# Hybrid decoder step: RWKV chain with full-array products and a block diagonal state, the last merge's gates issued behind the delta pair, the norm's mean taken from PSUM

## The chip, the cores and the metric

The kernel runs on one core of one Trainium2 chip. A core has five engines with instruction streams of their own: TensorE (PE, with PEld for its weight loads), VectorE (DVE), ScalarE (ACT), GpSimd (POOL) and SyncE (SP), which here issues the DMAs. The metric is the device time of one execution, in microseconds, the median of the runs; lower is better.

## What is computed

One inference step of a decoder with two layers, 512 prompt positions and 8 samples of 8 positions, together 576 columns, 1024 channels, float32.

```python
for l in range(DEPTH):                                    # 2
    x = layer_norm(ALPHA * x + 0.5 * swiglu(x, ffn1_w_in, ffn1_w_out))
    mix = token_mixing(x, ...)
    x = layer_norm(ALPHA * x + mix)
    x = layer_norm(ALPHA * x + 0.5 * swiglu(x, ffn2_w_in, ffn2_w_out))

# token_mixing: four branches read one projection of x
oa, ob, oc, om = rwkv7(pa), pool(pb), delta(pc), memory_attention(pm)
for i, o in enumerate((oa, ob, oc, om)):
    merged += sigmoid(pg[i]) * (o @ w_branch[i])
mix = merged @ w_out

# rwkv7, for each of 8 heads of 64 channels, over the positions
def step(s, inp):
    r_t, w_t, k_t, v_t, kk_t, a_t = inp
    sa = einsum('bhvk,bhk->bhv', s, kk_t)
    s = s * w_t - sa * (kk_t * a_t) + v_t * k_t
    return s, einsum('bhvk,bhk->bhv', s, r_t)
```

The delta branch has a recurrence of the same family, with heads of 128.

## The kernel before

Activations lie with channels on the partitions and the 576 columns along the free axis, in two halves of 288. Each dense product is made in split precision: a weight block of 128x512 is loaded by SyncE, cast by ScalarE to `fp32r` (L239) and its remainder formed by VectorE (L241); `mms` (L255) then issues three 128x288 products per block of 128 channels, 24 for eight blocks, 12 for four. There are 17,952 such products in a run.

A tile scheduler sets the order of each engine's stream from the program's dependencies. The program offers it two kinds of work: the chains of the branches, and **fill**, dense products that a generator (`fill_steps`, taken on by `advance`) hands out between the steps of the chains: the pool branch, attention, and the four merges of the branches. A merge (`merge`) makes for each of eight channel blocks j and each half a gate (24 products `pgt`, then a tanh into `th`), multiplies the branch with its `w_branch` (12 products `pbr`), and adds the two's product to `merged`. Merges come in the order i=1, then rows 12, 0 and 8 of the branch outputs; row 8, the delta branch, is the last and can start only when the second delta pair has stored its output in DRAM (`od`) and read it back (`oraw`, split into `O`). One gate is made ahead of its first `pbr`.

The RWKV branch runs over four pairs of heads, p = 0 to 3. `rwkv_prep` makes the tiles of a pair: `KR` holds for each chunk of 64 positions the scaled kk and r (L827, L828), `KB` the other factors (L825, L832); `pt` (L845) are their products, masked on VectorE into `MA` (L846); `inverse64` inverts the triangular part into a tile `W`. `rwkv_chain` then goes through eight chunks in turn. In each, `pr` sums `MA` times `VS` (the values) and `KR` times the state `S` (L916, L917), `rhs` is its copy on VectorE (L922), `psa` is the inverse times `rhs` (L891 in `rwkv_solve`), ScalarE writes it negated into `VS` (L893), `pu` is `KN` times `VS` (L929), from which VectorE makes the next `S` (L937); `pyc` collects the output (L921, L932), copied by ScalarE (L939). All of it is cut by head: two 64x64 or 128x64 products for each term. Between the steps, `rwkv_sample` hands out the steps of the samples' group (`pst`, `psel`, `pr8`, `py8`, `pu8`), one after the right-hand side, one after the solution or one at the chunk's end.

The delta branch (`delta_pair`, q = 0, 1) has a chain of its own (`pdz` L1258, `pdo` L1264, `pdu` L1284, L1328, `pdk`), ends with a norm on VectorE and ScalarE (`dVN`) and transposes the output by `pto` (L1356), after which `stash` stores it.

Each of the six norms (`out_norm`) collects statistics per half: at block j = 3 (`statistics`) the first four blocks are summed, `pm` is the product with ones, ScalarE scales it into `m` (L309), VectorE subtracts `m` from four blocks (L313), GpSimd subtracts it from later ones (L288). At the end VectorE makes the diagonals `dg` (L353) from which TensorE makes `prow` (L363).

## Time and profile before

| | |
|---|---|
| median of three runs | 3206.25 us (3206.08 to 3207.3) |
| the profiled execution | 3201.57 us |
| its span | 3199.9 us |
| mean granted clock of TensorE | 0.982 |
| TensorE busy | 3065.8 us, 96% |
| VectorE busy | 1934.4 us, 60% |
| ScalarE busy | 1283.6 us, 40% |
| GpSimd busy | 502.7 us, 16% |

The span is from the first to the last instruction of the profiled execution. Busy times are shares of that span; since products are pipelined, a busy TensorE also counts the overlap of its products. The timeline gives each instruction's start; the distance between starts is what a product takes from the stream.

### The profile page before, as it was taken

Reading aid. Unit: us, or ns where it says so; the run is one execution under the profiler, and the core shown is the slowest. Engines: PE = TensorE matmul, PEld = TensorE weight load, DVE = VectorE, ACT = ScalarE, POOL = GpSimd, SP = SyncE. Lnnn points to the kernel's source line nnn. Section 1 sums busy time; section 2 is a strip of 40 time slices with the busy share of each in tenths; the row PEclk is TensorE's granted clock in tenths of the full one; section 3 lists DMA queues with packets and bytes.
Section 4 is the critical chain, followed back from the end, with each engine's and each line's share of the span. In section 5 each row is a group of like instructions: output and inputs, shape, how many; then the busy total and the mean of one; then the engine's idle time right before and its main releaser. Section 6 shows DMA issues by size and latency. Waiting matters only on the chain. (4 is left out here: it accounts for less than half of the span.)

```text
span 3199.9 us, 61758 instructions
## 1 busy us (share of the span) xinstructions
PE 3065.8 (96%) x24224; PEld 2840.4 (89%) x24224; DVE 1934.4 (60%) x4405; ACT 1283.6 (40%) x3057; POOL 502.7 (16%) x819
## 2 busy tenths in 40 slices
PE   7999999999999989999999999999999998999998
PEld 7999988778888889899999998876888897989998
DVE  4335776466687756733673367775586887475337
ACT  3332544434535333432343235445345343344323
POOL 2002221102110114200220022211111101142002
PEclk9999999999999999999999999999999999999999
DMA  4232432142233233322332233322322332333222
GB/s 131 84 89 84 112 101 58 38 119 61 61 88 85 66 93 97 90 84 82 103 101 83 80 99 92 109 55 71 93 63 64 84 91 67 95 96 92 87 79 77
DMA packets 509902, 271.88 MB, mean 85 GB/s; under 512 B 45896, under 2 KB 500140, under 8 KB 509612
## 3 DMA queue, kind: packets, MB, share of 16 engines
q1 hardware_dynamic: 509612, 267.95, 30.4%
q8 instruction: 190, 3.11, 0.4%
q14 instruction: 100, 0.82, 0.1%
HBM read 248.12 MB, written 19.76 MB: 84 GB/s over the span
## 5 line engine op out<-in xcount | busy, mean ns | idle before, releaser
L241 DVE TENSOR_TENSOR w<-raw,w 128x512 fp32r<-128x512 f32 (+1 forms) x824 | 601.8, 733 | 371.8 <-ACT w L239 367.1
L239 ACT CAST w<-raw 128x512 fp32r<-128x512 f32 (+1 forms) x824 | 503.0, 614 | 642.3 <-PE po L255 233.8
L255 PE MATMUL pp<-X,w 128*128 128x288 f32 x3552 | 534.9, 303 | 7.2 <-ACT pv L555 2.8
L255 PEld LDWEIGHTS pp<-X,w 128*128 128x128 f32 x3552 | 485.8, 189 | 28.9 <-issue 11.8
L255 PE MATMUL pgt<-X,w 128*128 128x288 f32 x3072 | 505.6, 308 | 5.7 <-ACT th__29684 L1597 2.2
L255 PEld LDWEIGHTS pgt<-X,w 128*128 128x128 f32 x3072 | 433.2, 191 | 24.9 <-issue 7.9
L255 PE MATMUL pg<-X,w 128*128 128x288 f32 x3072 | 445.9, 297 | 5.4 <-DVE X L274 3.3
L255 PE MATMUL pu<-X,w 128*128 128x288 f32 x3072 | 438.5, 295 | 0.0
L255 PEld LDWEIGHTS pg<-X,w 128*128 128x128 f32 x3072 | 420.6, 189 | 10.7 <-DVE X L274 6.5
L255 PEld LDWEIGHTS pu<-X,w 128*128 128x128 f32 x3072 | 418.8, 188 | 0.1
L255 PE MATMUL po<-H,w 128*128 128x288 f32 x3072 | 414.0, 296 | 0.0
L255 PEld LDWEIGHTS po<-H,w 128*128 128x128 f32 x3072 | 409.6, 188 | 1.3
L255 PE MATMUL pbr<-O,w 128*128 128x288 f32 x1344 | 234.2, 310 | 23.9 <-ACT w L239 18.3
L255 PEld LDWEIGHTS pbr<-O,w 128*128 128x128 f32 x1344 | 193.7, 192 | 33.2 <-ACT w L239 21.2
L451 DVE TENSOR_TENSOR h<-h,pu 128x288 f32<-128x288 f32 x128 | 58.0, 453 | 259.5 <-PE pu L255 258.4
L288 POOL TENSOR_TENSOR T<-T,m 128x288 f32<-128x288 f32 x48 | 48.0, 1030 | 932.2 <-ACT m L309 931.9
L273 ACT CAST H<-h 128x288 fp32r<-128x288 f32 x128 | 55.2, 432 | 193.9 <-DVE h L451 193.8
L450 ACT ACTIVATE h<-pg 128x288 f32<-128x288 f32 x128 | 52.7, 411 | 179.2 <-PE pg L255 175.1
L255 PE MATMUL po<-mh,w 128*128 128x288 f32 x768 | 109.3, 304 | 4.3 <-DVE w L241 2.9
L255 PEld LDWEIGHTS po<-mh,w 128*128 128x128 f32 x768 | 106.6, 195 | 6.0 <-DVE w L241 3.3
L286 POOL TENSOR_TENSOR T<-X 128x288 f32<-128x288 f32 x96 | 92.3, 995 | 83.7 <-DVE X L274 55.3
L645 DVE TENSOR_TENSOR it<-W,iu 128x60 f32<-128x60 f32 (+24 forms) x372 | 96.3, 259 | 8.6
(1030 smaller groups left out, 3652.9 us busy)
## 6 DMA issues: line engine op xcount, KB each, us to landing
raw<-in_w_in_dram SPq DMA_DIRECT2D x280, 256.0 KB
raw<-in_ffn_w_in_dram SPq DMA_DIRECT2D x272, 256.0 KB
raw<-in_ffn_w_out_dram SPq DMA_DIRECT2D x160, 256.0 KB
raw<-in_w_branch_dram SPq DMA_DIRECT2D x48, 256.0 KB
raw<-in_w_out_dram SPq DMA_DIRECT2D x48, 256.0 KB
oraw<-od SPq DMA_DIRECT2D x28, 288.0 KB
kraw<-in_mem_w_kv_dram SPq DMA_DIRECT2D x16, 256.0 KB
kvr<-in_cache_mem_k_dram SPq DMA_DIRECT2D x16, 256.0 KB
```

Source lines behind the costliest of these rows:

```text
L239: nc.scalar.copy(w[:, 0, :m], raw)
L241: low.tensor_sub(w[:, 1, :m], raw, w[:, 0, :m].bitcast(F32))
L255: self.last = self.nc.tensor.matmul(ps, w[:, wp, d, :], X[k][:, part, sl], start=first and k == 0 and q == 0, stop=last and k == n - 1 and ...
L273: nc.scalar.copy(out[:, 0, sl], src)
L286: nc.gpsimd.tensor_add(t, self.X[j][:, 0, sl].bitcast(F32), self.X[j][:, 1, sl].bitcast(F32))
L288: nc.gpsimd.tensor_sub(t, t, self.stat[s]['m'])
L450: nc.scalar.activation(h, pg, AF.Silu)
L451: nc.vector.tensor_mul(h, h, pu)
L645: nc.vector.tensor_mul(w, d[:, :r, k:k + 1].to_broadcast([P, r, m]), u[:, k + 1:, k].unsqueeze(1).to_broadcast([P, r, m]))
```

## The change

Three things are changed.

**The RWKV chain.** The state of a head pair is one 128x128 tile `sb`, block diagonal, whose zeros are written once; the right-hand side goes into such a tile too, `rb`. `KR`'s two parts change places for the second head, so that the part of one head and the other's zero blocks fit the full product. The masked products are sorted into two tiles: `ML` for those with kk, `MR` for those with r; the inverse is written over the matrices in `ML`, and no tile `W` is used. `VS` gets zeros in its off-diagonal blocks from GpSimd. Each chunk then has six 128x128 products in place of its 64-wide ones. On the other engines an operation that covered both heads is two, one for each diagonal block: the copy into `rb`, the update of `sb`, the copy of `pyc`, and in the prep the writing of `KR` and the masking. The three kinds of sample steps all come at the chunk's end, and the sample group's own solution and output use the full products too. The final state is transposed whole.

**The last merge.** For row 8, five gates are made ahead instead of one; their products are issued only behind the last transpose `pto` (`self.pin`), and their `th` come from another tag of the pool.

**The norm's mean.** At j = 3 the four subtractions read the sum in PSUM, scaled in the same instruction, and not `m`; `m` is still made for GpSimd.

```diff
+        self.sb, self.rb = c.tile([P, P], F32, name="sb"), c.tile([P, P], F32, name="rb")
+        for t in (self.sb, self.rb):
+            nc.gpsimd.memset(t, 0.0)
...
+            for t in t4:
+                nc.vector.scalar_tensor_tensor(t, pz, -2.0 / D, t, ALU.mult, ALU.add)
         for i in range(0 if j == 3 else j, j + 1):
             ti = self.T[i // 2][:, i % 2, sl]
-            if i < 4:
-                nc.vector.tensor_sub(ti, ti, st['m'])
...
-        nc.vector.scalar_tensor_tensor(KR[:, :, 0], ch(k), col('rwkv_k_k'), ch(e1), ALU.mult, ALU.mult)
-        nc.vector.tensor_mul(KR[:, :, 1], ch(r), ch(ec2))
+
+        for h in range(2):
+            nc.vector.scalar_tensor_tensor(KR[R[h], :, 1 - h], ch(k)[R[h]], col('rwkv_k_k')[R[h]], ch(e1)[R[h]],
+                                           ALU.mult, ALU.mult)
+            nc.vector.tensor_mul(KR[R[h], :, h], ch(r)[R[h]], ch(ec2)[R[h]])
...
-                nc.vector.tensor_mul(MA[h][:, c:c + m].rearrange("p c k t -> p c (k t)"),
-                                     pt[:, :m * P].rearrange("p (c t) -> p c t", t=P),
-                                     mk.unsqueeze(1).to_broadcast([P, m, P]))
+                for kind, (dst, at) in enumerate(((ML, 1 - h), (MR, h))):
+                    nc.vector.tensor_mul(dst[:, c:c + m, at],
+                                         pt[:, :m * P].rearrange("p (c k t) -> p c k t", k=2, t=64)[:, :, at],
+                                         mk[:, 64 * kind:64 * kind + 64].unsqueeze(1).to_broadcast([P, m, 64]))
...
+        for h in range(2):
+            nc.gpsimd.memset(VS[R[h], :, R[1 - h]], 0.0)
...
-        DT = self.inverse64(lambda h: MA[h][R[1 - h], :, 0], lambda h: 64 * (1 - h))
+
+        DT = lambda h: ML[R[1 - h], :, 1 - h]
+        self.inverse64(DT, lambda h: 64 * (1 - h), DT)
...
+            nc.vector.tensor_copy(self.rb[R[1 - h], R[h]], rhs(h))
         psa = self.bank("psa")
-        for h in range(2):
-            nc.tensor.matmul(psa[R[1 - h], :64], DT[R[1 - h], c], rhs[R[1 - h]], start=True, stop=True)
-        for h in range(2):
-            nc.scalar.mul(VS[R[1 - h], c, R[h]], psa[R[1 - h], :64], -1.0)
+        nc.tensor.matmul(psa[:, :P], ML[:, c].rearrange("p k t -> p (k t)"), self.rb, start=True, stop=True)
+        for h in range(2):
+            nc.scalar.mul(VS[R[1 - h], c, R[h]], psa[R[1 - h], R[h]], -1.0)
...
+            nc.tensor.matmul(pr[:, :P], flat(ML[:, c]), VS[:, c], start=True, stop=c == 0)
+            if c:
+                nc.tensor.matmul(pr[:, :P], flat(KR[:, c]), S, start=False, stop=True)
+                nc.tensor.matmul(py[:, :P], S, flat(KR[:, c]), start=True, stop=False)
+            self.rwkv_solve(parts, c, lambda h: pr[R[1 - h], R[h]])
+            pu = self.bank("pu")
+            nc.tensor.matmul(pu[:, :P], KN[:, c], VS[:, c], start=True, stop=True)
+            nc.tensor.matmul(py[:, :P], VS[:, c], flat(MR[:, c]), start=c == 0, stop=True)
             for h in range(2):
-                if S is not None:
-                    nc.tensor.matmul(pr[R[1 - h], :64], KR[R[h], c, 0], S[R[h]], start=True, stop=False)
-                nc.tensor.matmul(pr[R[1 - h], :64], MA[h][R[h], c, 0], VS[R[h], c, R[h]], start=S is None,
-                                 stop=True)
-            if S is not None:
-                for h in range(2):
-                    nc.tensor.matmul(py[R[h], :64], S[R[h]], KR[R[h], c, 1], start=True, stop=False)
-            nc.vector.tensor_copy(rhs, pr[:, :64])
-            sample_step("wide")
-            self.rwkv_solve(parts, c, rhs)
-            sample_step("solve")
-            pu = self.bank("pu")
+                d = S[R[h], R[h]]
+                if c:
+                    nc.vector.scalar_tensor_tensor(d, d, pc[R[h], c:c + 1], pu[R[h], R[h]], ALU.mult, ALU.add)
+                else:
+                    nc.vector.tensor_copy(d, pu[R[h], R[h]])
             for h in range(2):
-                vs = VS[:, c, 64 * h:64 * h + 64]
-                nc.tensor.matmul(pu[R[h], :64], KN[:, c, 64 * h:64 * h + 64], vs, start=True, stop=True)
-            for h in range(2):
-                vs = VS[:, c, 64 * h:64 * h + 64]
-                nc.tensor.matmul(py[R[h], :64], vs, MA[h][:, c, 1], start=S is None, stop=True)
-            Sn = self.scr.tile([P, 64], F32, tag="S64", name="S64", bufs=2)
-            if S is None:
-                nc.vector.tensor_copy(Sn, pu[:, :64])
-            else:
-                nc.vector.scalar_tensor_tensor(Sn, S, pc[:, c:c + 1], pu[:, :64], ALU.mult, ALU.add)
-            S = Sn
-            nc.scalar.copy(y[:, 64 * c:64 * c + 64], py[:, :64])
-            sample_step("deep")
+                nc.scalar.copy(y[R[h], 64 * c:64 * c + 64], py[R[h], R[h]])
+            for kind in ("wide", "solve", "deep"):
+                sample_step(kind)
...
+                self.pin = nc.tensor.transpose(pt[:, d * P:(d + 1) * P], ON[:, c0 + d], self.ident)
...
-            self.mms(pg, gates[j], self.X, HALVES[s])
-            th = self.half("th_", "xf") if dst is None else dst
+            with self.tc.issue_after(self.pin.ins) if row == 8 else nullcontext():
+                self.mms(pg, gates[j], self.X, HALVES[s])
+            th = self.half("th_", "x" if row == 8 else "xf") if dst is None else dst
...
-            while todo and len(ahead) < (1 if j == 0 else 0):
+            while todo and len(ahead) < (0 if j else 5 if row == 8 else 1):
```

Line numbers grow by 3 to 14: L255 is L259 in the changed kernel, L241 is L245, L1356 is L1359.

TensorE in one chunk of the first head pair's chain, before (names as above; `pp` and `pgt` on L255 are fill):

```order
L916 MATMUL pr<-S_5618,KR 64x64
L917 MATMUL pr<-VS,MA_4376 64x64
L916 MATMUL pr<-S_5618,KR 64x64
L917 MATMUL pr<-VS,MA_4377 64x64
L921 MATMUL pyc<-KR,S_5618 64x64 x2
L255 MATMUL pp<-X,w 128x288 x2
L891 MATMUL psa<-rhs,W 64x64 x2
L255 MATMUL pp<-X,w 128x288 x5
L929 MATMUL pu<-VS,KN 64x64 x2
L932 MATMUL pyc<-MA_4376,VS 64x64
L932 MATMUL pyc<-MA_4377,VS 64x64
```

The same chain after (L929 to L932 make `pr` and `pyc`, L905 `psa`, L935 and L936 `pu` and the rest of `pyc`):

```order
L929 MATMUL pr<-VS,MA_4382 128x128
L259 MATMUL pgt<-X,w 128x288 x2
L931 MATMUL pr<-sb,KR 128x128
L932 MATMUL pyc<-KR,sb 128x128
L259 MATMUL pgt<-X,w 128x288 x3
L905 MATMUL psa<-rb,MA_4382 128x128
L259 MATMUL pgt<-X,w 128x288 x6
L935 MATMUL pu<-VS,KN 128x128
L936 MATMUL pyc<-MA_4383,VS 128x128
```

The product of `pr` with `VS` has moved up, ahead of two fills and the product with the state; the narrow products are six full ones, with three fills ahead of `psa` and six ahead of `pu`.

TensorE at the end of the second delta pair in the first layer, before:

```order
L255 MATMUL pbr<-O,w 128x288 x3
L255 MATMUL pgt<-X,w 128x288 x5
L1328 MATMUL pdu_12000<-dex,dKN 128x512
L1328 MATMUL pdu_12003<-dex,dKN 128x512
L1328 MATMUL pdu_12008<-dex,dKN 128x512
L1328 MATMUL pdu_12011<-dex,dKN 128x512
L255 MATMUL pgt<-X,w 128x288 x19
L255 MATMUL pbr<-O,w 128x288 x12
L255 MATMUL pgt<-X,w 128x288 x13
L1356 MATMUL pto<-ident,dVN 128x128 x9
L255 MATMUL pgt<-X,w 128x288 x11
L255 MATMUL pbr<-O,w 128x288 x12
```

After (`pp` are the pool and attention products):

```order
L259 MATMUL pp<-X,w 128x288 x47
L1261 MATMUL pdz<-drhs_11875,dDB 128x128
L259 MATMUL pp<-X,w 128x288
L1267 MATMUL pdo<-z,dMA 128x128
L1331 MATMUL pdu_11888<-dex,dKN 128x512
L1331 MATMUL pdu_11891<-dex,dKN 128x512
L1331 MATMUL pdu_11896<-dex,dKN 128x512
L1331 MATMUL pdu_11899<-dex,dKN 128x512
L1359 MATMUL pto<-ident,dVN 128x128 x9
L259 MATMUL pgt<-X,w 128x288 x120
L259 MATMUL pbr<-O,w 128x288 x60
L259 MATMUL pgt<-X,w 128x288 x24
```

All gate and branch products of the row-0 merge have left the stretch between the last `pdz` and `pto`; five whole gates stand behind `pto`, and then the branch products of five halves in a row.

VectorE in the mixing stage's norm of the first layer, second half, before:

```order
L345 TENSOR_SCALAR lnw<-pv 96x6
L241 TENSOR_TENSOR w<-raw,w 128x512
L313 TENSOR_TENSOR T<-T,m_14378 128x288 x4
L319 TENSOR_TENSOR s_14388<-q 128x288
L346 TENSOR_TENSOR lnw<-lnw 96x3
L293 SCALAR_TENSOR_TENSOR T<-po,T 128x288
L322 TENSOR_TENSOR s_14388<-s_14388,q 128x288
L347 SCALAR_TENSOR_TENSOR lnw<-lnw 96x3
```

And after:

```order
L349 TENSOR_SCALAR lnw<-pv 96x6
L245 TENSOR_TENSOR w<-raw,w 128x512
L315 SCALAR_TENSOR_TENSOR T<-pm_14264,T 128x288 x4
L350 TENSOR_TENSOR lnw<-lnw 96x3
L297 SCALAR_TENSOR_TENSOR T<-po,T 128x288
L323 TENSOR_TENSOR s_14278<-q 128x288
L351 SCALAR_TENSOR_TENSOR lnw<-lnw 96x3
L245 TENSOR_TENSOR w<-raw,w 128x512
```

The four operations on `T` read `pm` in PSUM; the residual (L293, now L297) and the small operations of the norm (`lnw`) stand ahead of the sums of squares (`s`).

## Rows read from the trace of the kernel before

**Rows 1.** The page: span, and busy time of each engine.
```profile
span 3199.9 us, 61758 instructions
...
PE 3065.8 (96%) x24224; PEld 2840.4 (89%) x24224; DVE 1934.4 (60%) x4405; ACT 1283.6 (40%) x3057; POOL 502.7 (16%) x819
```

**Rows 2.** TensorE's timeline, undisturbed products: start, duration (us), operation, count.
```profile
299.80 12.38 PE L255 MATMUL po<-H,w 128*128 128x288 f32 x92
```

**Rows 3.** TensorE's timeline through one chunk of an RWKV chain, 500.8 to 503.8 us.
```profile
500.83 0.66 PE L255 MATMUL pp<-X,w 128*128 128x288 f32 x3
501.42 0.28 PE L916 MATMUL pr<-S,KR 64*64 64x64 f32 x2
...
501.58 0.29 PE L917 MATMUL pr<-VS,MA 64*64 64x64 f32 x4
501.81 0.53 PE L255 MATMUL pp<-X,w 128*128 128x288 f32 x2
502.27 0.33 PE L891 MATMUL psa<-rhs,W 64*64 64x64 f32 x4
502.53 0.93 PE L255 MATMUL pp<-X,w 128*128 128x288 f32 x5
503.39 0.34 PE L929 MATMUL pu<-VS,KN 128*64 128x64 f32 x4
...
503.78 0.40 PE L255 MATMUL pp<-X,w 128*128 128x288 f32 x1
```

**Rows 4.** All engines' timeline, the same chunk: the operations between the products.
```profile
501.93 0.23 DVE L922 COPY rhs<-pr 128x64 f32<-128x64 f32 x1 [0.83 <-PE pr L917]
...
502.89 0.46 ACT L893 ACTIVATE VS<-psa 64x64 f32<-64x64 f32 x2
...
503.80 0.28 DVE L937 SCALAR_TENSOR_TENSOR S<-S,pc,pu 128x64 f32<-128x64 f32 x1 [0.21 <-PE pu L929]
```

**Rows 5.** TensorE's timeline, full 128x128 products in the delta branch.
```profile
1033.08 1.04 PE L1186 MATMUL ptk<-ident,dkq 128*128 128x128 f32 x8
...
1090.10 0.49 PE L1264 MATMUL pdo<-z,dMA 128*128 128x128 f32 x2
1090.34 0.64 PE L255 MATMUL pgt<-X,w 128*128 128x288 f32 x3
1090.83 0.67 PE L1284 MATMUL pdu<-zb,dKN 128*128 128x256 f32 x2
```

**Rows 6.** Groups by line, TensorE: busy us, mean ns of one, idle before, releasers.
```profile
L845 PE MATMUL pt<-KR,KB 64*128 64x128 f32 x288 | 34.7, 321 | 7.7 <-DVE KB L832 6.0 <-DVE MA L846 1.6
```

**Rows 7.** VectorE's timeline in a prep, the writing of `KR`.
```profile
534.92 0.82 DVE L827 SCALAR_TENSOR_TENSOR KR<-pa,par,e 128x576 f32<-128x576 f32 x1
```

**Rows 8.** TensorE's timeline at the second delta pair's end, idle time in brackets.
```profile
1130.98 0.46 PE L1258 MATMUL pdz<-drhs,dDB 128*128 128x128 f32 x2 [1.50 <-DVE drhs L1318]
...
1133.28 3.02 PE L1328 MATMUL pdu<-dex,dKN 64*128 64x512 f32 x8
...
1142.72 1.17 PE L1356 MATMUL pto<-ident,dVN 128*128 128x128 f32 x9 [0.39 <-DVE dVN L1342]
...
1154.58 3.44 PE L255 MATMUL pbr<-O,w 128*128 128x288 f32 x12 [9.23 <-ACT w L239]
```

**Rows 9.** VectorE's timeline in mixing's norm.
```profile
1253.09 4.02 DVE L313 TENSOR_TENSOR T<-T,m 128x288 f32<-128x288 f32 x4
...
1258.01 0.45 DVE L293 SCALAR_TENSOR_TENSOR T<-po,T 128x288 f32<-128x288 f32 x1
```

**Rows 10.** TensorE's waits from 1250 to 1295 us: total us, times, longest us.
```profile
PE prow L363 <- DVE dg L353: 5.0, 1, 5.0
PE po L255 <- DVE w L241: 1.4, 1, 1.4
```

**Rows 11.** Busy us by engine (PE, PEld, DVE, ACT, POOL), TensorE's granted clock, DMA.
```profile
1257.00:1287.40 30.40, 23.64 (x176) 22.61 (x174) 28.91 (x55) 13.51 (x27) 17.12 (x16) 1.00 0.42 122
1287.40:1294.40 7.00, 6.49 (x23) 5.90 (x24) 5.12 (x14) 2.55 (x5) 0.87 (x1) 0.51 0.15 41
```

More of the change, by code (lines that the diff above doesn't have):

```diff
@@ L836, in rwkv_prep @@
         nc.gpsimd.tensor_copy(pc[:, 8:16], ec2[:, SEQ:NT].rearrange("p (b t) -> p b t", t=LS)[:, :, LS - 1])
-        MA = [self.slot(f"MA{h}", F32, [P, NC_, 2, 64]) for h in range(2)]
+        ML, MR = MA = [self.slot(f"MA{k}", F32, [P, NC_, 2, 64]) for k in range(2)]
         for c in range(0, NC_, 4):
@@ L886, in rwkv_solve @@
         nc = self.nc
-        VS, DT = parts[3], parts[4]
+        (ML, MR), VS = parts[1], parts[3]
         R = (slice(0, 64), slice(64, 128))
+        for h in range(2):
+            nc.vector.tensor_copy(self.rb[R[1 - h], R[h]], rhs(h))
         psa = self.bank("psa")
+        nc.tensor.matmul(psa[:, :P], ML[:, c].rearrange("p k t -> p (k t)"), self.rb, start=True, stop=True)
         for h in range(2):
-            nc.tensor.matmul(psa[R[1 - h], :64], DT[R[1 - h], c], rhs[R[1 - h]], start=True, stop=True)
-        for h in range(2):
-            nc.scalar.mul(VS[R[1 - h], c, R[h]], psa[R[1 - h], :64], -1.0)
+            nc.scalar.mul(VS[R[1 - h], c, R[h]], psa[R[1 - h], R[h]], -1.0)
     def rwkv_chain(self, l, p, parts):
         nc = self.nc
-        KR, MA, KN, VS, DT, yg, pc = parts
+        KR, (ML, MR), KN, VS, DT, yg, pc = parts
         R = (slice(0, 64), slice(64, 128))
+        flat = lambda a: a.rearrange("p k t -> p (k t)")
         y = yg[:, 0, :NT]
+        S = self.sb
         sample = self.rwkv_sample(l, p, parts)
@@ L942, in rwkv_chain @@
+        so = self.half("so")[:, :64]
         for h in range(2):
-            nc.tensor.matmul(ptr[R[h], :64], S[R[h]], self.ident[R[h], R[h]], start=True, stop=True)
-        so = self.scr.tile([P, 64], F32, tag="r64", name="so", bufs=2)
-        nc.scalar.copy(so, ptr[:, :64])
+            nc.scalar.copy(so[R[h]], ptr[R[h], R[h]])
         nc.sync.dma_start(self.o['p_rwkv'][l, 0, 2 * p:2 * p + 2].rearrange("h v k -> (h v) k"), so)
@@ L952, in rwkv_sample @@
         nc = self.nc
-        KR, MA, KN, VS, DT, yg, pc = parts
+        KR, (ML, MR), KN, VS, DT, yg, pc = parts
         R = (slice(0, 64), slice(64, 128))
@@ L976, in rwkv_sample @@
         for h in range(2):
-            nc.tensor.matmul(pr[R[1 - h], :64], ks[R[h], 0], self.ident[R[h], R[h]], start=True, stop=False)
-            nc.tensor.matmul(pr[R[1 - h], :64], MA[h][R[h], 8, 0], VS[R[h], 8, R[h]], start=False, stop=True)
-        r0 = self.scr.tile([P, 64], F32, tag="r64", name="r8", bufs=2)
-        nc.vector.tensor_copy(r0, pr[:, :64])
+            nc.tensor.matmul(pr[R[1 - h], :64], ks[R[h], 1 - h], self.ident[R[h], R[h]], start=True, stop=False)
+            nc.tensor.matmul(pr[R[1 - h], :64], ML[R[h], 8, 1 - h], VS[R[h], 8, R[h]], start=False, stop=True)
         yield "solve"
-        self.rwkv_solve(parts, 8, r0)
+        self.rwkv_solve(parts, 8, lambda h: pr[R[1 - h], :64])
         nc.gpsimd.tensor_mul(SS, SS, pc[:, 8:16].unsqueeze(2).to_broadcast([P, NS, 64]))
@@ L985, in rwkv_sample @@
         py = self.bank("py8")
+        nc.tensor.matmul(py[:, :P], VS[:, 8], MR[:, 8].rearrange("p k t -> p (k t)"), start=True, stop=True)
         for h in range(2):
-            vs = VS[:, 8, 64 * h:64 * h + 64]
-            nc.tensor.matmul(py[R[h], :64], vs, MA[h][:, 8, 1], start=True, stop=True)
-        nc.vector.tensor_add(y[:, SEQ:NT], py[:, :64], ks[:, 1])
+            nc.vector.tensor_add(y[R[h], SEQ:NT], py[R[h], R[h]], ks[R[h], h])
         ex = self.slot("ex", F32, [P, 2, NS, 64], "iv")
```

4 lines of the change are left out of this document (1 added, 3 removed).

## The prediction

> **What bounds the kernel now.** I read the page's busy times first. TensorE is busy for 3065.8 of 3199.9 us, 96%, and no other engine comes near it [rows 1]. So an edit is worth one of two things: TensorE time that it adds or takes away, or an idle stretch of TensorE that it opens or closes. A microsecond saved on another engine counts only where TensorE waits for that engine. The unit of TensorE time is the dense 128x288 product: 92 of them in a row take 12.38 us, so one starts every 0.133 us [rows 2]. They fill the time in which the small chains wait, and I call them fill. The second view is TensorE's timeline through one chunk of the RWKV chain [rows 3], with the operations of VectorE and ScalarE between its products [rows 4]. The third is what full 128x128 products cost where before has them [rows 5]. The last three are the idle stretches that the change touches: before `pt` in a prep [rows 6, 7], the end of the second delta pair and the last merge [rows 8], and the mixing stage's layer norm [rows 9 to 11].
>
> **Part 1, TensorE's work in the chain.** The price of a group of small products is the distance between the fill on either side of it, less 0.133 us for each fill. The `pr`/`pyc` group: 501.81 - 500.83 = 0.98, less three fills, 0.58 us. `psa`: 502.53 - 501.81 less two fills, 0.46. `pu`/`pyc`: 503.78 - 502.53 less five fills, 0.58. Together 1.62 us a chunk [rows 3]. After has six full 128x128 products in their place. Such a product makes two records. Eight `ptk` records in a row last 1.04 us, of which some 0.28 is the last one's own length: (1.04 - 0.28)/7 = 0.11 a record, 0.22 a product. A lone `pdo` between fills costs 1090.83 - 1090.10 less three fills, 0.33, with what it waited [rows 5]. After has four of the six in two pairs and two alone, so a chunk costs 6 x 0.22 = 1.31 at least and 4 x 0.22 + 2 x 0.33 = 1.54 at most, and saves 0.08 to 0.31. I take 0.24, near the upper end since waits are priced apart below: for 64 chunks -15.5 us. Something comes back: the sample group's steps (five groups of 64-wide products in each of 8 chains, 40 in all) stood beside other 64-wide products and now stand between full ones. The four records of `psa` are over in 0.33 us and yet 0.46 pass between the fills [rows 3], 0.13 us for entering and leaving; I take 0.1 for each of the 40 steps, +4 us. **Term A: -11 us**, ends -15 and 0.
>
> The Trainium skill ("TensorEngine Tiling (Array Packing)", Tiling Modes) speaks against this part: it has 64x64 work run as four independent tiles, so that filling the array with zeros would throw time away. By that rule alone the twelve small products would cost three passes where after has six, 0.7 us a chunk more after the change, +42 us in all. The same section says that a change of mode drains the engine. This case's trace sides with the second sentence: the small products did not cost a fraction of a full one, they cost 1.62 us a chunk [rows 3]. Their price being measured, the first sentence gets no chance of its own.
>
> **Part 1, the chain's links.** Each chunk has three links on which TensorE waits for another engine, and fill stands in each. Before, one copy `rhs` (0.23), two `VS` copies (0.46) and one `S` update (0.28) [rows 4]. After, `rb` takes two copies, `VS` still two, `S` two updates. Times are counted from the end of the product that is read. *pr to psa*: the copy began 501.93 - 501.81 = 0.12 us after, and `psa` began 0.11 us after the copy's end. Two copies: 0.12 + 0.46 + 0.05 to 0.11 = 0.63 to 0.69, a little more with 128 columns. The cover is `pyc`, 0.22, and three fills, 0.40: 0.62. Wait 0.01 to 0.15. *psa to pu*: two copies 0.46, begun 0.12 to 0.36 after (502.89 - 502.53, behind a cast on ScalarE), 0.05 to `pu`: 0.63 to 0.87 against four fills, 0.53. Wait 0.10 to 0.34. *pu to pr*: 0.12 + 0.56 + 0.05 = 0.73, against `pyc`, `pr` from `VS` and two fills, 0.71; where a sample step stands there, nothing. So 0.11 to 0.5 us a chunk, and some links have five or six fills and wait for nothing. What queues behind these operations on VectorE is a 0.7 us weight split, which hits a link now and then, as it did before. I take 0.25 us for 64 chunks. **Term B: +16 us**, ends +3 and +31.
>
> **Part 1, the prep.** `KR` is written in four half-height pieces in place of two, each about as long as a whole one (0.82) [rows 7]: VectorE gets 1.6 us more before `KB` is ready, and `pt` already waits for it, 6.0 us in all [rows 6]: 1.5 us at each of two head pairs in both layers. At the first of the two there are also ten fills fewer ahead of `pt`, 1.3 us. If nothing hides it that is 2.9 + 1.6 us per layer, +9; other VectorE work may slip behind it, down to 0. The split of the mask products adds some 16 operations to eight preps, hidden by the fill after `pt`. **Term C: +5 us.**
>
> **Part 2, the last merge.** Before, TensorE waits 1.50 us for `drhs`, 0.39 for `pto` and 9.23 for the weights of `pbr`, which come after the round trip of the delta output through DRAM; that wait leaves the clock down, since twelve `pbr` then take 3.44 us instead of 12 x 0.133 = 1.6 [rows 8]. In all 12.9 us per layer. After, five gates (120 fills, 16 us) stand between `pto` and `pbr`, more than the 10.9 us from the end of `pto` to `pbr`. But they are pinned behind `pto`, and the other fill that stood between the last `pdz` and `pto` has moved ahead of `pdz`. From `pdz` to `pto` it is 1142.72 - 1130.98 = 11.7 us, a chain of VectorE and ScalarE work, of which TensorE then does only `pdz`, `pdo` and `pdu`: 0.24 + 0.24 + 3.0, and one fill. It stands idle for some 8.1 us there, and its clock will be down when it comes back, 2 to 3 us more: 10.1 to 11.1. So the wait does not go, it moves; 2 us per layer are won. **Term D: -4 us**, ends -10 and +6.
>
> **Part 3, the mean.** Four subtractions per half of a norm take 4.02 us from SBUF; the new form is that of the residual, one operand in PSUM, which takes 0.45 us [rows 9]: 1.8, so 2.2 us of VectorE less in each of twelve places. In the eight of the FFNs' norms TensorE waits for nothing of it: 0. In mixing's norm VectorE is the bound from 1253 to 1287: TensorE waits 1.4 us for a weight, then 5.0 for `dg` before `prow` [rows 10]. VectorE is busy for 28.9 of the 30.4 us up to there [rows 11], so what the two blocks save, 4.4 us, comes off these two waits. After the 5.0 us the granted clock is 0.51, the lower of its two levels, for 7 us, 3.4 us lost [rows 11]. With half the wait gone it may stay up. Per layer -4.4 without the clock and -7.8 with it. **Term E: -13 us**, ends -5 (if half of the saving is eaten by weights that VectorE then casts earlier) and -16.
>
> **Sum:** -11 + 16 + 5 - 4 - 13 = -7 us. The profiled execution took 3201.57 us, so it would become 3194.6; the median is 4.7 us above that execution, and the forecast of the median is 3206.25 - 7 = 3199.
>
> **Rivals.** *The links are covered* (B = +3): then the switches saved and the mean show alone, 3199 - 13 = 3186. For it: the fill was put there by a scheduler, and four or five fills are in most links. Against: the `psa` to `pu` link is short by any reading. *The links are bare* (B = +31, C = +9): two copies in a row where one stood, at each link, cost 0.5 us a chunk; 3199 + 15 + 4 = 3218, slower than before. It decides from 0.36 us a chunk on (B is then +23, and the sum zero); a weight split on VectorE in front of the second copy, 0.7 us in one link of three, is enough. *The gates pay in full*: the chain from `pdz` to `pto` is shorter once no fill stands in TensorE's queue in front of `pdo` and `pdu`, so idle and clock there come to 3 us: D = -19, 3184. Against: the operations in it are on VectorE and ScalarE. *The two small parts do nothing*: the clock falls after `prow` all the same (E = -9) and the idle time before `pto` is as long as the old one and its clock longer (D = +6): 3199 + 14 = 3213, or one of the two, 3205 to 3209.
>
> **How the numbers follow.** The likeliest case is the sum, 0.40, by itself 3193 to 3206, split 0.20 faster, 0.18 same, 0.02 slower; the bound is 0.2%, 6.4 us, about what a measurement of this kernel can tell from no change. Covered links 0.18 and gates in full 0.07, both faster. Bare links 0.18, slower. The small parts doing nothing 0.17, 0.15 of it same and 0.02 slower. So faster 0.45, same 0.33, slower 0.22. The range leaves out half of the bare links and the most of the gates in full: 3184 to 3217.
>
> **What would show it.** A: chunk groups without wait at 1.3 to 1.45 us between fills. B: idle time of TensorE in front of `psa` and `pu`, charged to `rb` and `VS`, 0.1 to 0.5 us a chunk. C: the wait of `pt` at pairs 1 and 2, 3 us in place of 1.5. D: no wait of `pbr` for a weight, but one of `pto` of about 8 us. E: the four operations in 1.8 us, the wait of `prow` at 2.5 us, and no low clock behind it. The forecast is wrong if `pto` waits under 3 us, if the links add over 0.4 us a chunk, or if VectorE's time in the preps rises by more than the `KR` pieces.

## The result, and the profile after

The changed kernel takes 3262.57 us (median of four runs, 3260.2 to 3268.35) against 3206.78 us for the kernel before: a ratio of 1.0173, 95% interval 1.0153 to 1.0193, 55.8 us slower. The forecast was 3199, the range 3184 to 3217. The profiled execution's span grew from 3199.9 to 3258.7 us.

The page of the changed kernel, span and busy time of each engine:

```profile
span 3258.7 us, 60661 instructions
...
PE 3115.1 (96%) x23432; PEld 2888.7 (89%) x23432; DVE 1962.9 (60%) x4613; ACT 1296.7 (40%) x3129; POOL 512.1 (16%) x837
```

Against [rows 1], TensorE is busy for 49 us more, although it has 792 instructions fewer. TensorE's waits over the whole execution (total us, times, longest us):

```profile
PE pt L853 <- DVE KB L839: 23.0, 4, 7.5
...
PE pto L1359 <- DVE dVN L1345: 10.9, 4, 5.1
PE prow L367 <- DVE dg L357: 10.9, 5, 3.3
...
PE pdu L1331 <- DVE dex L1326: 4.1, 2, 2.0
```

The wait of `pt` for `KB`, 6.0 us in [rows 6], is 23.0 us. The 9.23 us before `pbr` [rows 8] are gone, and `pto` waits longer.

To see where the 58 us of the profiled execution lie, I cut both traces at the same points of the program (first `pss`, first `pr` and first `pgm` of each head pair, the last `pto`, the last but one `prow` of the mixing norm) and split each stretch's time in four: fill, at 0.133 us each; idle time of TensorE; time lost at the lower granted clock, taken as half of the busy time in it; and the rest, which is what all other products cost TensorE. A wait of TensorE's weight loads (PEld) that the overlap of its products hides counts as rest and not as idle time. The sums over both layers, before to after:

```
stretch          time us          fills          idle us        low clock us   rest us
chains           212.2 -> 263.2    468 ->  598    0.5 ->  2.3    0.0 ->  0.0   149.4 -> 181.3
preps, outputs   663.2 -> 689.3   2728 -> 2704   30.2 -> 44.9   13.6 -> 28.7   256.7 -> 256.0
delta pairs      579.5 -> 582.5   2908 -> 2776   31.9 -> 46.8   10.2 -> 18.1   150.6 -> 148.3
merge 8, norm    334.0 -> 314.2   2114 -> 2138   32.8 -> 13.4    9.6 ->  6.7    10.5 ->   9.8
FFNs, others    1406.9 ->1405.1   9734 -> 9736   34.5 -> 31.7   14.0 -> 16.4    63.7 ->  62.1
```

The eight chains are 51 us longer, almost without idle time: 32 us of it are products of their own, 17 us are 130 more fills. Those fills are missing in the delta pairs, where the idle time rose by 15 us. The preps lose 15 us to idle time and 15 to the low clock. The last merge and the norm win 20 us.

The low clock's growth is too large in this table. The profiled execution of the kernel before had a mean granted clock of 0.982, while its 43 runs beside the experiments had 0.978 on average, which is up to 14 us more lost to the clock. In three experiments that leave the preps as they were (the gates alone, the mean alone, both), the low clock takes 20, 14 and 22 us of the preps and outputs, where the table has 13.6 for the kernel before.

One chunk of the first chain after the change, TensorE's timeline (the one to set beside [rows 3]):

```profile
504.66 0.49 PE L935 MATMUL pu<-VS,KN 128*128 128x128 f32 x2
504.99 0.39 PE L936 MATMUL pyc<-MA,VS 128*128 128x128 f32 x2
505.21 0.39 PE L929 MATMUL pr<-VS,MA 128*128 128x128 f32 x2
505.35 0.51 PE L259 MATMUL pgt<-X,w 128*128 128x288 f32 x2
505.84 0.49 PE L931 MATMUL pr<-sb,KR 128*128 128x128 f32 x2
506.16 0.39 PE L932 MATMUL pyc<-KR,sb 128*128 128x128 f32 x2
506.30 0.64 PE L259 MATMUL pgt<-X,w 128*128 128x288 f32 x3
506.89 0.49 PE L905 MATMUL psa<-rb,MA 128*128 128x128 f32 x2
507.14 1.03 PE L259 MATMUL pgt<-X,w 128*128 128x288 f32 x6
508.13 0.49 PE L935 MATMUL pu<-VS,KN 128*128 128x128 f32 x2
```

First come `pu`, `pyc` and the `pr` that reads `VS`, then `pr` and `pyc` with the state, then `psa`. Counted as in the prediction, from fill to fill: from 505.35 to 506.30 less two fills, 0.68 us for `pr` and `pyc`; from 506.30 to 507.14 less three, 0.44 for the lone `psa`. In [rows 3] the narrow `psa` cost 0.46. The group of `pu`, `pyc` and the first `pr`, from the four fills at 503.88 (shown further below) to 505.35, costs 0.94. A chunk comes to 2.06 us, where 1.3 to 1.45 had been said and [rows 3] have 1.62. The entry price that I had put down to the narrow form is there with the full form too. The weight loads show it, before and after (PEld rows of the two timelines, idle time in brackets):

```profile
502.27 0.19 PEld L891 LDWEIGHTS psa<-rhs,W 64*64 64x64 f32 x4 [0.16 <-DVE rhs L922]
```

```profile
506.89 0.30 PEld L905 LDWEIGHTS psa<-rb,MA 128*128 128x128 f32 x2 [0.18 <-DVE rb L903]
```

### The profile page after: what moved, and what is told of

It is laid out like the page before. It is cut to its first block, busy times and chain, and to the rows that moved or that the text cites. A ratio compares the mean times of both kernels' runs of the same rounds, so it can differ in the third digit from the quotient of the medians.

```text
span 3258.7 us, 60661 instructions
## 1 busy us (share of the span) xinstructions
PE 3115.1 (96%) x23432; PEld 2888.7 (89%) x23432; DVE 1962.9 (60%) x4613; ACT 1296.7 (40%) x3129; POOL 512.1 (16%) x837
## 4 chain that ended last, share of the span: by engine, by line
PE 75%; DVE 16%; issue 3%; ACT 3%; DMA 1%; POOL 0%; DVEq 0%; ACTq 0%; SPq 0%
PE po L259 13%; PE pg L259 12%; PE pu L259 12%; PE pp L259 10%; PE pgt L259 9%; PE pbr L259 4%; DVE it L649 2%; DVE w L245 2%; DVE W L651 2%; PE pt L853 1%; PE pu L935 1%; PE psa L905 1%; DMA raw<-in_w_in_dram 1%; PE pr L929 1%; ACT w L243 1%
## 5 line engine op out<-in xcount | busy, mean ns | idle before, releaser
L245 DVE TENSOR_TENSOR w<-raw,w 128x512 fp32r<-128x512 f32 (+1 forms) x824 | 599.2, 730 | 388.9 <-ACT w L243 384.1
L259 PE MATMUL pp<-X,w 128*128 128x288 f32 x3552 | 538.3, 304 | 6.9 <-ACT pc__27005 L559 2.1
L259 PEld LDWEIGHTS pp<-X,w 128*128 128x128 f32 x3552 | 490.1, 191 | 29.9 <-issue 16.0
L259 PE MATMUL pgt<-X,w 128*128 128x288 f32 x3072 | 508.0, 309 | 5.8 <-ACT th__29456 L1601 2.0
L259 PEld LDWEIGHTS pgt<-X,w 128*128 128x128 f32 x3072 | 435.4, 193 | 18.4 <-issue 5.1
L259 PE MATMUL pg<-X,w 128*128 128x288 f32 x3072 | 444.6, 296 | 7.3 <-DVE X L278 3.3
L259 PE MATMUL pu<-X,w 128*128 128x288 f32 x3072 | 438.6, 295 | 0.0
L259 PEld LDWEIGHTS pg<-X,w 128*128 128x128 f32 x3072 | 419.5, 188 | 12.6 <-DVE X L278 6.1
L259 PEld LDWEIGHTS pu<-X,w 128*128 128x128 f32 x3072 | 418.5, 188 | 0.1
L259 PE MATMUL po<-H,w 128*128 128x288 f32 x3072 | 413.7, 296 | 0.0
L259 PEld LDWEIGHTS po<-H,w 128*128 128x128 f32 x3072 | 409.3, 188 | 1.3
L259 PE MATMUL pbr<-O,w 128*128 128x288 f32 x1344 | 224.9, 306 | 4.9 <-DVE w L245 0.9
L259 PEld LDWEIGHTS pbr<-O,w 128*128 128x128 f32 x1344 | 190.2, 190 | 9.4 <-issue 1.8
L259 PE MATMUL po<-mh,w 128*128 128x288 f32 x768 | 107.3, 301 | 2.5 <-DVE T L297 2.5
L259 PEld LDWEIGHTS po<-mh,w 128*128 128x128 f32 x768 | 105.1, 193 | 3.8 <-DVE T L297 3.0
```

The lines of the kernel that those rows point to most:

```text
L245: low.tensor_sub(w[:, 1, :m], raw, w[:, 0, :m].bitcast(F32))
L259: self.last = self.nc.tensor.matmul(ps, w[:, wp, d, :], X[k][:, part, sl], start=first and k == 0 and q == 0, stop=last and k == n - 1 and ...
```

## The experiments

**One part at a time.** First the RWKV part alone: the diff of the two small parts undone.

```diff
-            for t in t4:
-                nc.vector.scalar_tensor_tensor(t, pz, -2.0 / D, t, ALU.mult, ALU.add)
...
-            while todo and len(ahead) < (0 if j else 5 if row == 8 else 1):
+            while todo and len(ahead) < (1 if j == 0 else 0):
```

> The changed kernel with parts 2 and 3 undone: only the RWKV chain and its prep are changed. Theory 1 (the whole loss is in the chain: full products that still wait at each link, and the longer prep): 3206.8 + 65 to 80 = 3272 to 3287, since the stretches of the last merge and norm were 9.9 us per layer shorter in the changed kernel's trace. Rival (the loss comes from the fill that parts 2 and 3 move, which leaves the chains and preps with other fill): about 3215.

3269.71 us, 1.0178 (1.0160 to 1.0197). By stretches the chains are 50.9 us longer and the preps and outputs 23.3, as in the changed kernel, and the merge stretch is as before. The whole loss is in the RWKV part: 60 us, a little under the range of theory 1. The two small parts then bring only 7 us on top of it (3269.71 to 3262.57). Their stretch is 20 us shorter there, but the delta pairs are 6 us longer and the preps 3.

The last merge's gates alone, in the kernel before:

```diff
-            while todo and len(ahead) < (1 if j == 0 else 0):
+            while todo and len(ahead) < (0 if j else 5 if row == 8 else 1):
```

> Kernel before with the last merge's five gates alone. Theory 1 (the wait moves from pbr to pto and half of it is won): 3206.8 - 4 to -12. Rival (the fill taken out of the delta chain's end costs as much in the delta pair as the merge gains): 3206.8 +- 3. Second rival (moved fill lengthens chains): 3215.

3199.07 us, 0.9961 (0.9944 to 0.9977). Theory 1, and at its better end. TensorE's timeline at the second delta pair's end, to set beside [rows 8]:

```profile
1126.82 0.46 PE L1258 MATMUL pdz<-drhs,dDB 128*128 128x128 f32 x2 [1.50 <-DVE drhs L1318]
...
1132.08 2.81 PE L255 MATMUL pgt<-X,w 128*128 128x288 f32 x19
1134.73 1.74 PE L255 MATMUL pbr<-O,w 128*128 128x288 f32 x12
1138.77 1.17 PE L1356 MATMUL pto<-ident,dVN 128*128 128x128 f32 x9 [2.31 <-DVE dVN L1342]
1139.70 16.13 PE L255 MATMUL pgt<-X,w 128*128 128x288 f32 x120
```

Before `pto` TensorE idles for 2.3 us, not 8: the gate and the branch products of the row-0 merge (19 and 12) stayed in front of it. The 120 fills behind it cover the round trip. In the changed kernel the same place reads

```profile
1161.99 0.46 PE L1261 MATMUL pdz<-drhs,dDB 128*128 128x128 f32 x2 [1.21 <-DVE drhs L1321]
...
1165.32 4.89 PE L1331 MATMUL pdu<-dex,dKN 64*128 64x512 f32 x8 [2.03 <-DVE dex L1326]
1175.07 2.15 PE L1359 MATMUL pto<-ident,dVN 128*128 128x128 f32 x9 [4.85 <-DVE dVN L1345]
1176.87 17.70 PE L259 MATMUL pgt<-X,w 128*128 128x288 f32 x120
1194.41 1.76 PE L259 MATMUL pbr<-O,w 128*128 128x288 f32 x12
```

and there TensorE waits for `drhs` 1.2, for `dex` 2.0 and for `dVN` 4.9 us, and has nothing between `pdu` and `pto`: the row-0 merge was used up earlier, by the chains.

The mean from PSUM alone, in the kernel before:

```diff
+            for t in t4:
+                nc.vector.scalar_tensor_tensor(t, pz, -2.0 / D, t, ALU.mult, ALU.add)
...
-            if i < 4:
-                nc.vector.tensor_sub(ti, ti, st['m'])
```

> Kernel before with the mean from PSUM alone. Theory 1 (VectorE is the bound in mixing's norm): -9 to -15 us, 3192 to 3198, the wait of prow down from 5.0 to 2.5 us in each layer. Rival (other VectorE work moves in): within 3 us of before.

3208.64 us, 0.9986 (0.9972 to 1.0): nearer the rival. TensorE's waits in the first layer's mixing norm (total us, times, longest):

```profile
PE prow L363 <- DVE dg L353: 3.6, 1, 3.6
PE po L255 <- DVE T L293: 1.3, 1, 1.3
```

The 5.0 us of [rows 10] are 3.6. For `po` TensorE waited 1.4 us there, and 0.7 us more for a residual, which [rows 10] do not list; now it is 1.3. Over both layers the stretch lost 2.5 us of idle time.

Both small parts, the chain as before (the two diffs above together):

> Kernel before with parts 2 and 3, the chain as before. If the parts are independent: the sum of what the two give alone; by theory 1 3185 to 3195. If the rival holds (the gates' gain is given back in the delta pair): what the mean gives alone.

3188.58 us, 0.9921 (0.9902 to 0.9940). The stretch of merge and norm is 19.9 us shorter, as much as in the changed kernel, where it was 19.8. This kernel beats both.

**What a product costs.** Each chunk's `psa` and `pu` issued twice, first in the kernel before, then in the changed one:

```diff
         nc.tensor.matmul(psa[:, :P], ML[:, c].rearrange("p k t -> p (k t)"), self.rb, start=True, stop=True)
+        nc.tensor.matmul(psa[:, :P], ML[:, c].rearrange("p k t -> p (k t)"), self.rb, start=True, stop=True)
...
             nc.tensor.matmul(pu[:, :P], KN[:, c], VS[:, c], start=True, stop=True)
+            nc.tensor.matmul(pu[:, :P], KN[:, c], VS[:, c], start=True, stop=True)
```

> Kernel before with each chunk's psa and pu issued twice, the same product into the same place: 17 more pairs of 64-wide products in each chain, standing right behind the first, so without a wait or a switch of their own. It measures what the narrow products themselves cost. Theory 1 (two narrow products run side by side and a pair takes about half a full product): 17 x 0.11 = 1.9 us of TensorE time a chain, 15 us in all. Rival (narrow products cost as much as full ones and the array's form makes no difference): 17 x 0.22 = 3.7 us a chain, 30 in all.

> Changed kernel with each chunk's psa and pu issued twice: 17 more full products in each chain. Theory 1: 17 x 0.22 = 3.7 us of TensorE time a chain, 30 us in all, twice what the pairs cost in the kernel before. Rival (what a product group costs is its entry alone): under 1 us a chain in both.

TensorE's timeline with the narrow `psa` doubled:

```profile
501.75 0.53 PE L255 MATMUL pp<-X,w 128*128 128x288 f32 x2
502.21 0.33 PE L891 MATMUL psa<-rhs,W 64*64 64x64 f32 x4
502.38 0.28 PE L893 MATMUL psa<-rhs,W 64*64 64x64 f32 x4
502.59 0.66 PE L255 MATMUL pp<-X,w 128*128 128x288 f32 x3
```

502.59 - 501.75 less two fills is 0.57, against 0.46 in [rows 3]: a second pair of narrow products costs 0.12 us. With the full `psa` doubled, and below it the same `psa` of the changed kernel:

```profile
505.64 0.64 PE L259 MATMUL pgt<-X,w 128*128 128x288 f32 x3
506.32 0.46 PE L905 MATMUL psa<-rb,MA 128*128 128x128 f32 x2
506.62 0.39 PE L906 MATMUL psa<-rb,MA 128*128 128x128 f32 x2
506.76 0.78 PE L259 MATMUL pgt<-X,w 128*128 128x288 f32 x4
```

```profile
502.98 0.64 PE L259 MATMUL pgt<-X,w 128*128 128x288 f32 x3
503.67 0.46 PE L905 MATMUL psa<-rb,MA 128*128 128x128 f32 x2
503.88 0.77 PE L259 MATMUL pgt<-X,w 128*128 128x288 f32 x4
```

506.76 - 505.64 less three fills is 0.72, against 503.88 - 502.98 less three, 0.50: a second full product costs 0.22 us. Over all chains the rest rose by 14.5 us in the one and by 28.3 in the other: for 136 additional terms 0.107 us a narrow pair and 0.208 us a full product. Theory 1, near its numbers (15 and 30). The narrow products of two heads do run beside each other (in the first trace the two heads' records start 7 ns apart), and the full product that replaces a pair costs twice the pair. A full product also has 128 columns where each narrow one has 64; the runs do not separate this from the pairing.

The whole times do not show this factor of two: 3224.57 and 3283.89 us, a single run each, 18 us above the kernel before (3206.74 beside it) and 21 above the changed kernel. In the second the chains grew by 28 us, and the idle time of the preps fell by some 10. The two prices rest on the chains alone.

**The doubled operations.** The changed kernel with one operation for both heads in the copy to `rb`, the update of `sb` and the copy of `pyc`. It leaves out the placing of the second head's block, and `VS` is written with zeros; that the values have no part in the time is not shown by this run:

```diff
-        for h in range(2):
-            nc.vector.tensor_copy(self.rb[R[1 - h], R[h]], rhs(h))
+        nc.vector.tensor_copy(self.rb[:, :64], rhs(None))
...
-            nc.scalar.mul(VS[R[1 - h], c, R[h]], psa[R[1 - h], R[h]], -1.0)
+            nc.scalar.mul(VS[R[1 - h], c, R[h]], psa[R[1 - h], R[h]], 0.0)
...
-            for h in range(2):
-                d = S[R[h], R[h]]
+            d = S[:, :64]
```

> Changed kernel in which the copy into rb, the update of sb and the copy of pyc are one operation for both heads again (they then go to the first 64 columns, and VS is written with zeros, so the chain's values are not those of the reference); products and order rule as in the changed kernel. Theory 1 (the chain's loss is the products' own time and the restart after a wait): the chains keep most of it, 3262 - 5 to -12. Rival, the one of the prediction (the doubled operations leave the links bare): the chains fall back to about those of before, 3262 - 25 to -35.

3218.56 us against 3262.57, 44 us less: beyond both numbers, and in the rival's direction. But the links never were bare as the rival has it: the chains' idle time went from 2.3 to 1.8 us. What went out of the chains is fill, 598 to 464 (17.8 us), and 11 us of rest. Ten of these 11 are waits all the same, of the weight loads: their idle time in the chains fell from 54.1 to 43.8 us, most of it in front of `psa` and of the `pr` that reads `sb`. The fill stands in preps, outputs and delta pairs, where idle time fell by 20 us and the low clock's share by 12. The wait of `pt`:

```profile
PE pt L853 <- DVE KB L839: 9.8, 4, 3.5
```

It fell from 23.0 to 9.8 us though nothing in the prep was changed.

The opposite, in the kernel before: narrow products, and each of the three operations made in two.

```diff
-            nc.vector.tensor_copy(rhs, pr[:, :64])
+            for h in range(2):
+                nc.vector.tensor_copy(rhs[R[h]], pr[R[h], :64])
```

> Kernel before, its narrow products kept, with the copy rhs, the update of S and the copy of pyc made in two operations, one for each head. Theory 1 (the longer links draw fill into the chains, which is then missing in preps and the delta pairs): +10 to +30 us, no idle time in the chains, some 10 us of fill more in them. Rival (the links are covered by what fill there is): within 5 us.

3241.24 us, 1.0098 (1.0081 to 1.0114), 31 us slower: theory 1. This kernel computes what the kernel before does. The chains' idle time is 0.2 us; fills in them rose from 468 to 632, 21.8 us, more than twice what I had said, and their rest by 17.6 us: 6 us of it are waits of the weight loads, the others come with groups of products that the scheduler took apart. The fill missing elsewhere shows less than theory 1 has it: idle time in preps, outputs and delta pairs rose by only 5 us, 4 of them the wait of `pt` (6.0 to 10.2).

**KR in four pieces.** The changed kernel with two operations of full height; it leaves out the change of places for the second head:

```diff
-        for h in range(2):
-            nc.vector.scalar_tensor_tensor(KR[R[h], :, 1 - h], ch(k)[R[h]], col('rwkv_k_k')[R[h]], ch(e1)[R[h]],
-                                           ALU.mult, ALU.mult)
-            nc.vector.tensor_mul(KR[R[h], :, h], ch(r)[R[h]], ch(ec2)[R[h]])
+        nc.vector.scalar_tensor_tensor(KR[:, :, 0], ch(k), col('rwkv_k_k'), ch(e1), ALU.mult, ALU.mult)
+        nc.vector.tensor_mul(KR[:, :, 1], ch(r), ch(ec2))
```

> Changed kernel with KR written by two operations of full height as before (its blocks then lie in the wrong places for the second head). Theory 1 (the four half-height pieces are what pt waits for): the wait of pt for KB falls from 23.0 us to about 10, and with it low clock behind pt: 3262 - 13 to -25. Rival (the wait comes from the fill that the scheduler put elsewhere): the wait stays above 18 us, 3262 - 5 at most.

3227.64 us, 35 us less than the changed kernel, more than theory 1 gave. The wait:

```profile
PE pt L851 <- DVE KB L837: 7.7, 4, 2.4
```

It is 7.7 us. In the preps and outputs idle time fell by 9 us and the low clock's share by 12; the delta pairs won 8 and 4 us more. And the four pieces put into the kernel before (its blocks left where they were):

> Kernel before with each of the two operations that write KR cut into its two halves of 64 partitions. Theory 1: the wait of pt for KB rises from 6.0 us to 12 or more, with low clock behind it: +8 to +25 us. The prediction's term C for the same thing: +5.

3233.25 us, 1.0071 (1.0046 to 1.0095), 23.6 us slower, at the high end. The wait alone tells little of that:

```profile
PE pt L847 <- DVE KB L834: 9.3, 4, 3.2
```

It is 9.3 us, 3.3 more than in [rows 6], less than the 12 expected. In the preps of the profiled execution idle time rose by 7 us and the low clock took 23 us more; its span, 3239.3 us, lies near the top of the six runs (3214.7 to 3241.0), so 23 is more than the median's share. The mean granted clock of all six runs is 0.974, that of the kernel before beside them 0.977; this is at most 10 us of the 24. Nor do the 23 us follow the wait of `pt`: over 540 to 547 us, right behind the wait at the second head pair, the granted clock is 0.54, and 0.51 in the kernel before. The longest new stretch is 697 to 711 us, at 0.52 where the kernel before has 1.00, and the last wait of `pt` ahead of it ended at 657.

**Products alone.** The two edits of the changed kernel together, which leaves of the RWKV part the full products, the masking in pieces, the zeros and the sample steps at the chunk's end:

> Changed kernel with one operation for both heads in the chain and KR written by two operations (blocks in wrong places, VS written with zeros): of the change to the RWKV branch only the full products, the masking in two pieces and the zeros are left, beside parts 2 and 3. The kernel with parts 2 and 3 alone took 3188.6. Theory 1 (the full products cost 49 x 0.10 = 4.9 us of TensorE time a chain by themselves): 3205 to 3222. Rival (only the doubled operations cost): 3185 to 3193.

3213.94 us, 1.0016 (1.0005 to 1.0027), 25 us above the kernel with parts 2 and 3 alone: theory 1. In the chains the rest is 21 us above that kernel's, with two fills' difference and 2.5 us of idle time. That is half of the 4.9 us a chain (39 in all) that theory 1 named. So what is left, the full products above all, is the floor of the loss, some 25 us; the masking, the zeros and the sample steps were not run apart. Against the changed kernel with two `KR` operations (3227.64) the doubled operations are worth 14 us here, not 44: 128 fills left the chains, and the idle time of preps, outputs and delta pairs together hardly changed.

**A further try.** The kernel with parts 2 and 3, and the second `KR` operation on GpSimd:

```diff
-        nc.vector.tensor_mul(KR[:, :, 1], ch(r), ch(ec2))
+        nc.gpsimd.tensor_mul(KR[:, :, 1], ch(r), ch(ec2))
```

> Kernel before with parts 2 and 3 and the second of the two KR operations given to GpSimd, which has time: VectorE's way to KB is 0.75 us shorter at each prep. If pt waits for KB alone: its wait falls from 6.0 to about 3 us and the time from 3188.6 to some 3184. Rival (GpSimd's product is slower than VectorE's three steps and pt then waits for it): no gain, or up to 8 us lost.

3192.12 us, 0.9948 (0.9934 to 0.9963): no gain over 3188.58, the rival. `pt` waits 5.7 us in place of 6.0, and still for `KB` on VectorE, not for GpSimd; why the shorter way brings nothing stays open.

## Why the prediction was wrong, point by point

**Term A (-11 us) had the wrong sign**, and its step is the one that took 0.58 + 0.46 + 0.58 us for the price of the narrow form and 0.22 us for that of a full product. The first price holds three entries into the stream of fill, and I priced the second almost without any. The second copy of `psa` costs 0.12 us narrow and 0.22 full, of the 0.46 and 0.44 of a lone group. Take the entries out on both sides and a chunk has six pairs at 0.107 before, 0.64 us, and six full products at 0.208 after, 1.25. What remains for entries is 0.98 us of 1.62 before and 0.81 of 2.06 after: the products cost 0.61 us more, the entries 0.17 less, together 0.44 us a chunk, 28 us in 64 chunks. 32 were seen in the changed kernel, 21 with the doubled operations gone. So an entry price of the narrow form does exist, but it is small beside what the full products add. The row for a full product's entry, the lone `pdo` at 0.33, was in my own bounds, and I set it aside because waits were to be priced apart; the narrow groups' 1.62 us had them in.

Here the Trainium skill ("TensorEngine Tiling (Array Packing)", Tiling Modes) was dismissed too soon. It has tiles operate independently of each other; the runs with doubled products agree, at 0.107 us for two narrow ones against 0.208 for a full one. By that rule alone I had worked out +42 us; that working took all twelve narrow products for 64x64, and those of `pu` [rows 3] and of the second `pyc` are 128x64. Its other sentence, that a change of mode drains the engine, agrees with the trace of the kernel before. In its chains the first weight load of `pr`, which mostly waits for nothing there, starts 0.14 to 0.17 us after the fill's last load has ended (44 places), about as that of `pu`, which waits; the fill behind a narrow group starts 0.03 to 0.07 us after the group's last load (170 places). In the changed kernel the fill behind a full group starts some 0.08 us before the end of the group's last load (148 places), and what stands in front of a full group shrinks with the link: for the `pr` that reads `sb` it is 0.21 us in the median with two operations and 0.01 with one, for `psa` 0.18 and 0.12. So both prices exist: the narrow form pays at each change, the full one for its waits.

**Term B (+16 us) had the right cause, looked for its price in one place, and was too small.** The doubled operations are worth 31 us when put into the kernel before, 44 when taken out of the changed one, and 14 when taken out of it with `KR` in two operations. In the links themselves the term was not far off: TensorE's idle time there rose by only 1.8 us, but 10 us of waiting went with the doubled operations from its weight loads. The step that failed is the cover: the scheduler covered the longer links with 130 more fills, and I booked fill as free. Fill is a fixed amount (17,952 products in both kernels), so what stands in a chain is missing somewhere else: the delta pairs idled 15 us more and the preps 15. How much of that is the missing fill alone stays open. With the doubled operations taken out of the changed kernel, 134 fills leave the chains and the idle time outside them falls by 20 us; with `KR` in two operations, 128 leave and it hardly changes; in the kernel before, 164 come in and it grows by 5 us. The missing fill was dear only together with the longer prep. The rival of the bare links had the direction and no more: it priced 0.5 us a chunk as a wait in place, and gave 3218.

**Term C (+5 us): the operations were right, the wait behind them was not.** The four pieces do last 0.81, 0.74, 0.82 and 0.76 us, as was said; VectorE and TensorE in the prep of the second head pair:

```profile
536.16 0.81 DVE L833 SCALAR_TENSOR_TENSOR KR<-pa,par,e 64x576 f32<-64x576 f32 x1
536.89 0.74 DVE L835 TENSOR_TENSOR KR<-pa,e 64x576 f32<-64x576 f32 x1
...
537.65 0.82 DVE L833 SCALAR_TENSOR_TENSOR KR<-pa,par,e 64x576 f32<-64x576 f32 x1
538.38 0.76 DVE L835 TENSOR_TENSOR KR<-pa,e 64x576 f32<-64x576 f32 x1
...
541.31 6.35 PE L853 MATMUL pt<-KR,KB 64*128 64x128 f32 x36 [4.04 <-DVE KB L839]
```

Taking them away brings 35 us, putting them in costs 24. The step that failed is "If nothing hides it that is 2.9 + 1.6 us per layer, +9": the wait of `pt` rose by 17 us, to 4.0 us at the second head pair of each layer and 7.5 at the third, and fell by 13 when the doubled operations alone were taken out. So the term left out what the chain's longer links add to the same wait. It also put the clock at nothing. Behind the wait at the second head pair the lower level lasted longer than before; before and after (columns: window, length, busy time and count of PE, PEld, DVE, ACT, POOL, then PEclk, DMA share, GB/s):

```profile
540.00:546.80 6.80, 6.80 (x44) 5.51 (x43) 5.21 (x13) 2.20 (x5) 3.00 (x4) 0.50 0.16 39
```

```profile
541.30:552.50 11.20, 11.19 (x77) 9.63 (x77) 8.88 (x21) 2.65 (x7) 4.30 (x8) 0.54 0.30 72
```

By the mean granted clock of all runs (0.974 with the four pieces, 0.981 without) the lower level is up to 24 of the 35 us in the changed kernel, and up to 10 of the 24 in the kernel before. There it did not come right behind the waits of `pt`, as the experiment shows, so what brings it stays open.

**Term D (-4 us) was pessimistic by itself:** alone it gives -10 to -13. The step that failed is the 8.1 us of idle time before `pto`; they were read from the order of the changed kernel, where the RWKV part had drawn the fill out of that stretch, and booked to this part. In the changed kernel itself it came out nearly as said: 2.0 and 4.9 us idle between `pdz` and `pto`, and behind them nine `pto` take 2.15 us and 120 gates 17.70, against 1.17 and 16.13 with the gates alone. There the two small parts together give 7 us, where D and E had said 17. (From the end of `pto` to `pbr` [rows 8] have 10.7 us, not 10.9; nothing hangs on it.)

**Term E (-13 us) was too large:** alone 0 to -9 us (0.9972 to 1.0). The four operations take less than I said, 1.54 us, here at 1280 us of the changed kernel's VectorE timeline, with TensorE's wait for `dg` behind it:

```profile
1280.05 1.54 DVE L315 SCALAR_TENSOR_TENSOR T<-pm,T 128x288 f32<-128x288 f32 x4
```

```profile
PE prow L367 <- DVE dg L357: 3.3, 1, 3.3
```

But of the 4.4 us of a layer only 1.4 came off the wait of `prow` and 0.8 off those of `po`; "what the two blocks save, 4.4 us, comes off these two waits" is the sentence that failed. VectorE took other work in the time: with the mean alone `dg` starts 9.5 us after the four operations have ended, and 8.3 us in the kernel before.

**The sum.** In medians, products alone 25, doubled operations 31 and `KR` 24 (each of the two in the kernel before), the two small parts -21 together: 59, and 56 was measured. That nearness is luck. The RWKV part alone costs 60 us, not the 80 of its three pieces, and the small parts bring 7 us beside it, not 21; the two misses cancel. Taken out of the changed kernel the doubled operations and the pieces of `KR` give 44 and 35, but only 49 together.

Fills inside the first chain, in its whole length, as the windows of the dense line show them before and after (window, length, busy time and count of PE, of PEld, then clock and DMA):

```profile
484.58:510.46 25.88, 14.16 (x65) 9.20 (x64) 1.00 0.21 52
```

```profile
480.84:512.78 31.94, 15.73 (x81) 11.24 (x79) 1.00 0.21 51
```

64 weight loads of fill before, 79 after, in a chain that is 6 us longer.

## What to carry to other kernels

Price a small product by issuing it twice and taking the difference: the distance between its neighbours also holds the change of form and the wait in front of it. Where a scheduler hides a chain behind a fixed amount of other work, a longer link shows little idle time of TensorE in the chain; look at its weight loads, and where that work has become short, and count the covering work before and after. Compare granted clocks over all runs and not from one profiled execution of each kernel, and test a change of several parts one part at a time: here two parts alone won 21 us and the third alone lost 60, and together they lost 56.

## What the runs showed of the hardware that I had not expected

Two narrow products, each 64 or 128 rows by 64 columns, cost 0.107 us as a pair behind a group that is already running, against 0.208 us for one full 128x128 product. A change between 128x128 products and narrow ones has a price in the weight loads even where nothing is waited for: 0.14 to 0.17 us in front of the narrow `pr` (44 places) and 0.03 to 0.07 us in front of the fill behind a narrow group (170 places). Behind a full 128x128 product the fill's load starts some 0.08 us before the end of the load ahead (148 places), and in front of one it starts up to 0.01 us late where the link is short (the `pr` that reads `sb`, one operation per link) and 0.21 us late where it waits. An operation of VectorE on 64 partitions takes as long as the same one on 128: 0.81 us for 64x576 and 0.82 for 128x576 [rows 7].
